# Float32r activation tiles of the 256-column products moved to byte 416 of a 512-byte block, on one Trainium2 core

## The chip, the cores and the metric

One Trainium2 chip, one of its cores, one launch of one program. The metric is device time in microseconds of that program, as the median of three runs. Parameters come from HBM, and the result goes back there.

## The reference

Two blocks in a row on 256 tokens of width 1024, in float32. The matrix products of both make up nearly all the work:

```
# first block
mod = silu(c) @ w_mod + b_mod                       # scale, shift, gate
h, hc = modulate(x, ...), modulate(ctx, ...)
q, k, v, g ... = split(h @ w_in)                    # retention and difference attention
x = x + mod[2] * (concat([ret, diff]) @ w_out)
h2 = modulate(x, ...)
x = x + mod[5] * peer_ffn(h2)                       # see below

# peer_ffn: 8 heads choose 16 of 128 * 128 experts for each token
q = h2 @ w_query;  s = q . sub_keys
experts, gate = top-k of the sums of two halves of s, softmax
act = gelu(expert_u[experts] . h2)
out = sum over the chosen: gate * act * expert_v[experts]

# second block, two layers
x = x + ((b * conv(c * u)) @ w_out)                 # layer 0: b, c, u = split(h @ w_in)
x = x + block_attention(h, keys and values of x)    # layer 1
x = x + softmax(q . k_mem) v_mem @ w_o              # both layers
x = x + (silu(h @ w_g) * (h @ w_u)) @ w_down        # both layers, 22 chunks of 128
out = rms_norm(x)
```

The peer layer is computed densely: all 16,384 experts are scored against all tokens, and the gates, zero for the experts that weren't chosen, are multiplied in.

## The kernel before, in words

Activations are kept transposed: a tile of [128, 8, 256] holds 8 chunks (`KC`) of 128 features on the partitions, and 256 tokens (`T`) along the free side. A float32 value is split into two float32r parts, `hi` (the cast) and `lo` (what the cast leaves), and a product of float32 matrices is three float32r products: hi by hi, weights' lo by hi, weights' hi by lo.

Weights come in blocks of [128, 1024]: one DMA on SyncE's queue into `raw` (`raw`), the cast to `whi` on ScalarE (L111) and the subtraction to `wlo` on VectorE or GpSimd (L115, `lo_plan` says which). `block` (L149) takes one such block, and `mm3` (L127) issues its 3 x 8 = 24 matmuls at L137, hi-hi for all chunks, then lo-hi, then hi-lo, all into one PSUM tile:

```
order = [(s, i) for s in range(3) for i in range(n)]
a, b = ((wh, xh), (wl, xh), (wh, xl))[s]
self.matmul = nc.tensor.matmul(out, a, b, start=..., stop=...)
```

The first operand, here 128 columns of weights, is loaded into the array (a record PEld of its own in the profile), the second, here the 256 tokens of one chunk, is streamed through it. Each matmul has a weight load of its own. Where a product is wanted with the tokens on the partitions (`natural_steps`, L172), the roles are turned round: 128 tokens of the activation are loaded, and 256 columns of weights are streamed. The expert sum of the peer (L942) streams 512 columns of weights over 128 tokens.

Stages follow each other in this order: conditioning and mixer (`mixer`, from the start to 310 us), peer (`peer`; queries and scores of the experts from 310, the filling of the slots by gates among the expert scores until 788, the expert sum until 1143), convolution (`conv_mixer`), memory attention (`mem_attn`), feed-forward (`swiglu`, L1275 ff.), block attention (`moba`), memory attention and feed-forward of layer 1. In between, steps of work for later stages (keys and values of the memory, `fill`) are handed out at places that a table names (`PLACES`, `at`).

The tiles that the change touches are the streamed activations: `hh`/`hl` of `gained` (L253), which the convolution, both memory attentions, both feed-forwards and the keys of the block attention stream; `h2h`/`h2l` in `peer`; `cath`/`catl` in `mixer`; `oh`/`ol` in `mem_attn` and `moba`; `ch`/`cl` in `conv_mixer`; `fh`/`fl` in `swiglu`; `hqh`/`hql` in `moba`. All are float32r, taken from pools one tile after another, and a matmul streams 1024 bytes of each partition at a time, so that all chunks of a tile start on the same byte of a 512-byte block. That byte is given by what the pools hold ahead of the tile: 256 for `hh`, `hl`, `fh`, `fl`, and for `oh`, `ol` of the memory attentions; 352 in the convolution (`hh`, `hl`, `ch`, `cl`); 288 for `hqh`, `hql` and the block attention's `oh`, `ol`; 384 for `cath`, `catl`; 224 for `h2h`, `h2l`. The weight tiles `whi` and `wlo` all start at byte 224 of such a block, as do their slices of 128 columns (512 bytes).

Of the kernel before, what the change touches and what calls it, by code (L numbers as in the profile page):

```python
# [16 lines left out]
F32R = mybir.dt.float32r  # L17
# [8 lines left out]
P = 128  # L26
T = 256
D = 1024
KC = 8
EPS = 1e-6  # L30
NCH = 128
NKC_FF = 22
# [31 lines left out]
ROUTE = 14, 15, 16  # L64
LOWEST = -3.0e38

G_NORM1, G_NORM2, G_MIX, G_MEM, G_MEMKV, G_FFN, G_KV, G_FINAL = 0, 1, 2, 4, 6, 8, 10, 11


class Build:  # L70
# [23 lines left out]
    def after(self, ins, other):  # L94
# [2 lines left out]
                               mybir.DependencyInfo(mybir.DependencyClass.NoSync, mybir.DependencyReason.DATA),  # L97
                               reason="order")


    def raw(self, src, pool=None, tag="raw", bufs=3):
        t = (pool or self.wpool).tile([P, 1024], F32, name=tag, tag=tag, bufs=bufs)
# [147 lines left out]
            nc.vector.scalar_tensor_tensor(h[1][:, k, cols], t, Bv[:, k:k + 1],  # L250
                                           h[0][:, k, cols].bitcast(F32), op0=OP.add, op1=OP.subtract)

    def gained(self, pool, x, gi, name="h"):  # L253

        hi = pool.tile([P, KC, T], F32R, name=name + "h", tag=name + "h", bufs=1)
        lo = pool.tile([P, KC, T], F32R, name=name + "l", tag=name + "l", bufs=1)
        for k in range(KC):
            self.gain_chunk(x[:, k], gi, k, hi[:, k], lo[:, k])
        return hi, lo
# [173 lines left out]
    def mixer(self):  # L433
        nc, io, tc = self.nc, self.io, self.tc
        with ExitStack() as ctx:
            self.banks(ctx, "mix")
            pool = self.pool(ctx, "mix")
# [55 lines left out]
            qk_g = self.load(pool, "qk_g", [P, 2])  # L493
            nc.vector.tensor_scalar(qk_g[:, 0:1], qk_g[:, 0:1], 0.125, None, op0=OP.mult)
            nc.vector.tensor_scalar(df_n, df_n, 1.0 - LAM_INIT, None, op0=OP.mult)
            cat = (pool.tile([P, KC, T], F32R, name="cath"), pool.tile([P, KC, T], F32R, name="catl"))

            toks = [(h[0][:, :, i * P:(i + 1) * P], h[1][:, :, i * P:(i + 1) * P]) for i in range(4)]

# [198 lines left out]
    def peer(self):  # L698
        nc, io = self.nc, self.io
        with ExitStack() as ctx:  # L700
# [1 line left out]
            big = self.pool(ctx, "slots")  # L702
            pool = self.pool(ctx, "peer")
            slots = big.tile([P, NCH, T], F32, name="slots")
            h = (pool.tile([P, KC, T], F32R, name="h2h"), pool.tile([P, KC, T], F32R, name="h2l"))
            space = slots[:, FREE:, :].rearrange("p c t -> p (c t)")
            at = [0]

# [412 lines left out]
    def mem_attn(self, l, kv):  # L1121
        nc, io = self.nc, self.io
        with ExitStack() as ctx:
            pool = self.pool(ctx, f"mem{l}")
            kT, v = kv
            h = self.gained(pool, self.x, G_MEM + l)
            cat = (pool.tile([P, KC, T], F32R, name="oh"), pool.tile([P, KC, T], F32R, name="ol"))
            r = None

            def query(hd):  # L1130
                nonlocal r
                o = self.psum([P, 2, T])
                q = pool.tile([P, 2, T], F32, name="q", tag="q", bufs=1)
                qh, ql = (pool.tile([P, 2, T], F32R, name="q" + c, tag="q" + c, bufs=3) for c in "hl")
                for i in range(2):
                    self.block(o[:, i], io["mem_wq"][l, 2 * hd + i], h, late=hd == i == 0)
                if hd == 0:
                    r = self.tracked_norm(pool, "nr", tables=l == 0)
                nc.vector.scalar_tensor_tensor(q, o, 1.0 / 16.0, r[:, None, :].to_broadcast([P, 2, T]),
                                               op0=OP.mult, op1=OP.mult)  # L1140
                nc.scalar.copy(qh, q)
                getattr(nc, QLO).tensor_sub(ql, q, qh)
                return qh, ql

            def weigh(hd, q):
                ps = []
                for tt in range(2):
                    s = self.psum([P, T], "sc")
                    t = slice(tt * P, (tt + 1) * P)
                    self.mm3(s, [(q[0][:, i, t], q[1][:, i, t], kT[0][:, 2 * hd + i], kT[1][:, 2 * hd + i])  # L1150
                                 for i in range(2)])
                    ps.append(self.softmax(pool, s, T, "ms"))
                return ps

            def turned(ps):
                pT = [pool.tile([P, 2, 2, P], F32R, name="pT" + c, tag="pT" + c, bufs=2) for c in "hl"]
                for tt, p in enumerate(ps):
                    tr = self.psum([P, 2, P], "aux")
                    for j in range(2):
                        nc.tensor.transpose(tr[:, j], p[:, j * P:(j + 1) * P], self.ident)  # L1160
                    nc.scalar.copy(pT[0][:, :, tt], tr)
                    nc.vector.tensor_sub(pT[1][:, :, tt], tr, pT[0][:, :, tt])
                return pT

            def apply(hd, pT):
                o = self.psum([P, 2, T], "aux")
                for i in range(2):
                    c = slice((2 * hd + i) * P, (2 * hd + i + 1) * P)
                    self.mm3(o[:, i], [(v[0][:, j, c], v[1][:, j, c], pT[0][:, j], pT[1][:, j]) for j in range(2)])
                nc.scalar.copy(cat[0][:, 2 * hd:2 * hd + 2], o)  # L1170
                nc.vector.tensor_sub(cat[1][:, 2 * hd:2 * hd + 2], o, cat[0][:, 2 * hd:2 * hd + 2])

            self.at(f"m{l}")
            qs = [query(0), query(1)]
            self.at(f"mq{l}")
            ps = weigh(0, qs[0])
            for hd in range(3):
                if hd < 2:
                    qs.append(query(hd + 2))
                self.at((f"mh{l}", hd))  # L1180
                pT = turned(ps)
                ps = weigh(hd + 1, qs[hd + 1])
                apply(hd, pT)
            self.at(f"me{l}")

            def rest():
                pT = turned(ps)
                yield
                apply(3, pT)

            self.residual_l(io["mem_wo"][l], cat, 6, rest())
# [27 lines left out]
    def conv_mixer(self, hook):  # L1219
        nc, io = self.nc, self.io  # L1220
        with ExitStack() as ctx:
            pool = self.pool(ctx, "conv")
            cw = self.load(pool, "conv_w", [P, KC, 3])
            h = self.gained(pool, self.x, G_MIX)
            cat = (pool.tile([P, KC, T], F32R, name="ch"), pool.tile([P, KC, T], F32R, name="cl"))

            def gate(m, o, b):
                cu = pool.tile([P, 2, T], F32, name="cu", tag="cu", bufs=2)
                nc.vector.tensor_mul(cu, o, r[:, None, :].to_broadcast([P, 2, T]))
                z = pool.tile([P, T], F32, name="z", tag="z", bufs=2)  # L1230
                nc.gpsimd.tensor_mul(z, cu[:, 0], cu[:, 1])
                y = pool.tile([P, T], F32, name="cy", tag="cy", bufs=2)
                nc.vector.tensor_scalar(y, z, cw[:, m, 2:3], None, op0=OP.mult)
                nc.vector.scalar_tensor_tensor(y[:, 1:], z[:, :T - 1], cw[:, m, 1:2], y[:, 1:],
                                               op0=OP.mult, op1=OP.add)
                nc.vector.scalar_tensor_tensor(y[:, 2:], z[:, :T - 2], cw[:, m, 0:1], y[:, 2:],
                                               op0=OP.mult, op1=OP.add)
                nc.gpsimd.tensor_mul(y, y, r)
                t = pool.tile([P, T], F32, name="ct", tag="ct", bufs=2)
                nc.vector.tensor_mul(t, b, y)  # L1240
                nc.scalar.copy(cat[0][:, m], t)
                nc.vector.tensor_sub(cat[1][:, m], t, cat[0][:, m])

            self.adder = getattr(nc, CADD)
            for k in range(KC):
                self.track(self.x[:, k], k)
            self.adder = nc.gpsimd
            for m in range(KC):
                self.at(("c", m))
                if m == HOOK:  # L1250
                    hook()
                o = self.psum([P, 2, T], "sc" if m < 2 else "mm")
                for i, c in enumerate((1, 2)):
                    self.block(o[:, i], io["conv_wi"][8 * c + m], h, late=m == i == 0)
                    if m == 1 and i == NORM1:
                        r = self.tracked_norm(pool, "nr", tables=True)
                b = self.psum([P, T])
                self.block(b, io["conv_wi"][m], h)
                if m == 0:
                    first = o, b  # L1260
                    continue
                if m == 1:
                    gate(0, *first)
                gate(m, o, b)
            self.at("ce")
            self.residual_l(io["conv_wo"], cat)

    def swiglu(self, l):
        nc, io = self.nc, self.io
        with ExitStack() as ctx:  # L1270
            pool = self.pool(ctx, f"ffn{l}")
            h = self.gained(pool, self.x, G_FFN + l)
            self.at(f"f{l}")
            act = (pool.tile([P, NKC_FF, T], F32R, name="fh"), pool.tile([P, NKC_FF, T], F32R, name="fl"))
            for m in range(NKC_FF):  # L1275
                o = self.psum([P, 2, T])
                for i in range(2):
# [58 lines left out]
    def moba(self):  # L1336
        nc, io = self.nc, self.io
        with ExitStack() as ctx:
# [34 lines left out]

            self.at("bk")
            kT = pool.tile([P, KC, T], F32, name="k")
            hq = [pool.tile([P, KC, T], F32R, name="hq" + c) for c in "hl"]

            def query(hd):
                return plain(io["moba_wq"][hd], hq, 128.0 ** -0.5)
# [9 lines left out]
                ahead = t  # L1389
                self.gain_chunk(self.x[:, hd], G_MIX + 1, hd, hq[0][:, hd], hq[1][:, hd])  # L1390

            cat = (pool.tile([P, KC, T], F32R, name="oh"), pool.tile([P, KC, T], F32R, name="ol"))

            def weigh(hd, q):
                ps = []
# [219 lines left out]
```

## Time and profile before

| | |
|---|---|
| median of 3 runs | 1922.86 us (1920.68 to 1924.4) |
| profiled execution, own time | 1923.66 us |
| its span | 1921.8 us |
| mean granted TensorE clock | 0.984 |
| TensorE busy | 1853.1 us (96%), 13488 matmuls |
| VectorE, ScalarE, GpSimd busy | 1329.4, 967.3, 538.4 us |
| DMA | 335.12 MB, mean 174 GB/s |

The profile shows one execution. PE is TensorE's matmuls, PEld its weight loads, DVE VectorE, ACT ScalarE, POOL GpSimd, SP SyncE. A matmul's record runs from its start until its last result is written and overlaps with the next ones, so that a mean of 280 ns says nothing of how fast they follow each other; that is read from starts, or from a stretch without idle time divided by its matmuls. The chain of waits goes back from the last instruction to what released it, or to the instruction ahead of it on its engine; asked for a stretch, it shows what ended that stretch.

### The profile page before, as it was taken

To read this page: it belongs to the slowest core of one execution; us is meant where nothing else is said; L and a number is where in the kernel's file an instruction comes from. 1 tells how busy PE (TensorE), PEld (TensorE's weight loads), DVE (VectorE), ACT (ScalarE), POOL (GpSimd) and SP (SyncE) were. 2 spreads that over 40 slices of the span, in tenths; PEclk is the share of its full clock that TensorE was granted. 3 is DMA by queue.
4 is the path that set the end of the run, shared out by engine and by line. 5 is a ranking of instruction groups with operands and counts; after the bars stand their busy time and mean duration, and the time that the engine had idled before them with its cause. 6 is when DMAs were issued, how large, how long until landed. Compare 5 with 4: busy or idle time off the path is not lost.

```text
span 1921.8 us, 34715 instructions
## 1 busy us (share of the span) xinstructions
PE 1853.1 (96%) x13488; PEld 1739.1 (90%) x13488; DVE 1329.4 (69%) x2594; ACT 967.3 (50%) x1517; POOL 538.4 (28%) x289
## 2 busy tenths in 40 slices
PE   6799999999999999999999998999999999999997
PEld 4697788999999999888888878999999998999997
DVE  8988965995555666765555568666765578767664
ACT  5655534445554444454544454455554545555453
POOL 2511115787666666200000004232000222110001
PEclk8999999999999999999999998999999999999999
DMA  7663434454444444655555555544555553535553
GB/s 262 219 229 119 134 131 158 165 186 166 155 148 153 150 154 154 242 188 195 196 189 196 195 196 171 185 160 150 196 189 187 187 175 117 176 114 190 190 188 121
DMA packets 99764, 335.12 MB, mean 174 GB/s; under 512 B 12400, under 2 KB 13456, under 8 KB 99216
## 3 DMA queue, kind: packets, MB, share of 16 engines
q1 hardware_dynamic: 98160, 330.68, 49.7%
q8 instruction: 106, 1.74, 0.4%
q10 hardware_dynamic: 1440, 2.23, 0.3%
q14 instruction: 58, 0.48, 0.1%
HBM read 329.59 MB, written 3.28 MB: 173 GB/s over the span
## 4 chain that ended last, share of the span: by engine, by line
PE 85%; DVE 8%; ACT 2%; issue 2%; DMA 2%; POOL 1%; SPq 0%; DVEq 0%; ACTq 0%; POOLq 0%
PE mm L137 52%; PE pair L942 18%; PE mm L172 4%; PE pair L879 3%; PE fill L172 2%; PE fill L137 2%; DVE wlo L115 1%; PE sc L137 1%; PE aux L137 1%; DVE mlo L115 1%; DMA mraw<-w_mod 0%; DVE roper L379 0%; DMA raw<-w_mod 0%; PE sc L614 0%; PE aux L619 0%
## 5 line engine op out<-in xcount | busy, mean ns | idle before, releaser
L111 ACT CAST whi<-raw 128x1024 fp32r<-128x1024 f32 x564 | 591.8, 1051 | 568.9 <-PE mm L137 294.0
L115 DVE TENSOR_TENSOR wlo<-raw,whi 128x1024 fp32r<-128x1024 f32 x389 | 487.3, 1254 | 283.1 <-PE pair L942 130.0
L115 POOL TENSOR_TENSOR wlo<-raw,whi 128x1024 fp32r<-128x1024 f32 x175 | 425.1, 2430 | 296.3 <-PE mm L137 195.6
L137 PE MATMUL mm<-hh,whi 128*128 128x256 f32 (+1 forms) x1184 | 179.9, 289 | 5.6 <-DVE ct L1240 4.4
L219 POOL TENSOR_TENSOR acc<-acc,accsq 128x256 f32<-128x256 f32 x42 | 40.1, 954 | 500.0 <-ACT accsq L217 500.0
L137 PE MATMUL mm<-hl,whi 128*128 128x256 f32 (+1 forms) x1184 | 176.8, 287 | 1.0 <-DVE hl L264 1.0
L137 PE MATMUL mm<-hh,wlo 128*128 128x256 f32 (+1 forms) x1184 | 175.9, 286 | 0.0
L137 PE MATMUL mm<-h2h,whi 128*128 128x256 f32 x1152 | 171.1, 291 | 4.1 <-ACT h2h L249 4.1
L137 PEld LDWEIGHTS mm<-hh,whi 128*128 128x128 f32 x1184 | 156.6, 190 | 10.6 <-issue 6.9
L137 PE MATMUL mm<-h2l,whi 128*128 128x256 f32 x1152 | 161.7, 283 | 0.0
L137 PE MATMUL mm<-h2h,wlo 128*128 128x256 f32 x1152 | 161.7, 283 | 0.0
L942 PE MATMUL pair<-whi,actl 128*128 128x512 f32 x512 | 158.2, 390 | 1.8 <-DVE actl L935 1.8
L942 PE MATMUL pair<-whi,acth 128*128 128x512 f32 x512 | 158.1, 390 | 0.7 <-ACT acth L934 0.7
L137 PEld LDWEIGHTS mm<-hl,whi 128*128 128x128 f32 x1184 | 155.4, 190 | 3.6 <-DVE hl L264 1.7
L137 PEld LDWEIGHTS mm<-hh,wlo 128*128 128x128 f32 x1184 | 155.3, 190 | 3.5 <-issue 1.5
L942 PE MATMUL pair<-wlo,acth 128*128 128x512 f32 x512 | 157.9, 389 | 0.2 <-DVE wlo L115 0.2
L137 PEld LDWEIGHTS mm<-h2h,whi 128*128 128x128 f32 x1152 | 149.8, 193 | 5.0 <-ACT h2h L249 4.8
L137 PEld LDWEIGHTS mm<-h2l,whi 128*128 128x128 f32 x1152 | 148.6, 192 | 0.0
L137 PEld LDWEIGHTS mm<-h2h,wlo 128*128 128x128 f32 x1152 | 148.6, 192 | 0.0
L863 DVE TENSOR_TENSOR ohA<-fill,selT 128x256 f32<-128x256 f32 x128 | 53.7, 420 | 94.5 <-PE pair L879 91.0
L942 PEld LDWEIGHTS pair<-whi,actl 128*128 128x128 f32 x512 | 95.7, 188 | 22.5 <-DVE actl L935 2.9
L942 PEld LDWEIGHTS pair<-wlo,acth 128*128 128x128 f32 x512 | 96.0, 188 | 20.7 <-DVE wlo L115 0.6
(408 smaller groups left out, 3165.6 us busy)
## 6 DMA issues: line engine op xcount, KB each, us to landing
raw<-peer_u SPq DMA_DIRECT2D x128, 512.0 KB, 3.5
raw<-peer_v SPq DMA_DIRECT2D x128, 512.0 KB, 3.5
raw<-ffn_gu SPq DMA_DIRECT2D x88, 512.0 KB, 3.5
raw<-ffn_dn SPq DMA_DIRECT2D x44, 512.0 KB, 3.5
raw<-w_mod SPq DMA_DIRECT2D x64, 256.0 KB, 3.9
raw<-conv_wi SPq DMA_DIRECT2D x24, 512.0 KB, 3.5
raw<-mem_wk SPq DMA_DIRECT2D x16, 512.0 KB, 4.5
mraw<-w_mod SPq DMA_DIRECT2D x16, 512.0 KB, 6.2
```

What stands on the lines that cost most here:

```text
L111: self.hi_copy = nc.scalar.copy(hi, raw)
L115: (nc.vector if plan == "v" else nc.gpsimd).tensor_sub(lo, raw, hi)
L137: self.matmul = nc.tensor.matmul(out, a, b, start=first and j == 0, stop=last and j == 3 * n - 1)
L172: self.matmul = nc.tensor.matmul(outs[i // 2][:, i % 2], a[:, k, :], b[:, w], start=k == 0 and s == 0 and i % 2 == 0, stop=k == 7 and s == ...
L219: self.adder.tensor_add(self.acc, self.acc, self.last)
L863: nc.vector.tensor_tensor(A, iota[:, None, :].to_broadcast([P, 2, P]), selT[:, 1, t:t + 2, None].to_broadcast([P, 2, P]), op=OP.is_equal)
L879: nc.tensor.matmul(o[:, 2 * j + i], A[:, i], Bt[:, i], start=True, stop=True)
L942: nc.tensor.matmul(acc[th][:, dh], x[:, tsl], wt[:, dh * 512:dh * 512 + 512], start=c == 0 and s == 0, stop=c == NCH - 1 and s == 2)
```

## The change

A helper `placed` takes a tile that is 128 elements (512 bytes) longer in each partition and hands out the part that begins `at` elements into it; the tiles named above come from it. With `at` x 4 bytes ahead, each of them starts on byte 416: 256 + 160, 352 + 64, 288 + 128, 224 + 192; for `cath` the room is 8 elements, which moves `catl` behind it by as much, 384 + 32 both. `hh`/`hl` of the mixer, streamed 512 columns at a time for the most part, stay at 224, as do the weights and the expert sum's activations. On all five engines' queues the instructions and their order are the same as before.

```
+ROOM = 128
+    def placed(self, pool, name, at, k=KC, room=ROOM, **kw):
+        t = pool.tile([P, k * T + room], F32R, name=name, **kw)
+        return t[:, at:at + k * T].rearrange("p (k t) -> p k t", k=k)
...
-    def gained(self, pool, x, gi, name="h"):
-        hi = pool.tile([P, KC, T], F32R, name=name + "h", tag=name + "h", bufs=1)
-        lo = pool.tile([P, KC, T], F32R, name=name + "l", tag=name + "l", bufs=1)
+    def gained(self, pool, x, gi, name="h", at=40):
+        hi = self.placed(pool, name + "h", at, tag=name + "h", bufs=1)
+        lo = self.placed(pool, name + "l", at, tag=name + "l", bufs=1)
...
-            cat = (pool.tile([P, KC, T], F32R, name="cath"), pool.tile([P, KC, T], F32R, name="catl"))
+            cat = self.placed(pool, "cath", 8, room=8), self.placed(pool, "catl", 0, room=0)
...
-            h = (pool.tile([P, KC, T], F32R, name="h2h"), pool.tile([P, KC, T], F32R, name="h2l"))
+            h = self.placed(pool, "h2h", 48), self.placed(pool, "h2l", 48)
...
-            cat = (pool.tile([P, KC, T], F32R, name="oh"), pool.tile([P, KC, T], F32R, name="ol"))
+            cat = self.placed(pool, "oh", 40), self.placed(pool, "ol", 40)
...
-            h = self.gained(pool, self.x, G_MIX)
-            cat = (pool.tile([P, KC, T], F32R, name="ch"), pool.tile([P, KC, T], F32R, name="cl"))
+            h = self.gained(pool, self.x, G_MIX, at=16)
+            cat = self.placed(pool, "ch", 16), self.placed(pool, "cl", 16)
...
-            act = (pool.tile([P, NKC_FF, T], F32R, name="fh"), pool.tile([P, NKC_FF, T], F32R, name="fl"))
+            act = self.placed(pool, "fh", 40, NKC_FF), self.placed(pool, "fl", 40, NKC_FF)
...
-            hq = [pool.tile([P, KC, T], F32R, name="hq" + c) for c in "hl"]
+            hq = [self.placed(pool, "hq" + c, 32) for c in "hl"]
...
-            cat = (pool.tile([P, KC, T], F32R, name="oh"), pool.tile([P, KC, T], F32R, name="ol"))
+            cat = self.placed(pool, "oh", 32), self.placed(pool, "ol", 32)
```

## Rows read from the trace of the kernel before

**Rows 1.** Page, parts 1 and 4: busy time by engine, chain that ended last.

```profile
PE 1853.1 (96%) x13488; PEld 1739.1 (90%) x13488; DVE 1329.4 (69%) x2594; ACT 967.3 (50%) x1517; POOL 538.4 (28%) x289
...
PE 85%; DVE 8%; ACT 2%; issue 2%; DMA 2%; POOL 1%; SPq 0%; DVEq 0%; ACTq 0%; POOLq 0%
PE mm L137 52%; PE pair L942 18%; PE mm L172 4%; PE pair L879 3%; PE fill L172 2%; PE fill L137 2%; DVE wlo L115 1%; PE sc L137 1%; PE aux L137 1%; DVE mlo L115 1%; DMA mraw<-w_mod 0%; DVE roper L379 0%; DMA raw<-w_mod 0%; PE sc L614 0%; PE
```

**Rows 2.** Busy time in stretches: peer's scores, slots filled, first feed-forward.

```profile
core 0: us, PE busy (x) PEld busy (x) DVE busy (x) ACT busy (x) POOL busy (x), PEclk, DMA share, GB/s
362.00:452.00 90.00, 90.00 (x753) 90.00 (x752) 82.00 (x321) 43.34 (x53) 72.93 (x32) 1.00 0.51 179
458.00:788.00 330.00, 330.00 (x2791) 329.96 (x2790) 201.12 (x491) 159.05 (x255) 226.74 (x95) 1.00 0.44 154
1345.00:1455.00 110.00, 110.00 (x945) 110.00 (x944) 76.61 (x103) 57.63 (x82) 0.00 (x0) 1.00 0.56 192
```

**Rows 3.** Chain within one stretch each (start us, us, what): pieces without a wait.

```profile
399.92 20.16 PE mm L137 x168
...
1342.98 117.14 PE mm L137 x1004
...
1730.38 117.72 PE mm L137 x1009
...
1635.97 17.80 PE mm L137 x151
...
1211.18 25.63 PE mm L137 x216
...
1541.91 10.18 PE mm L172 x86
```

**Rows 4.** Timeline of PE, 291.8 to 299.5 us (start us, us, what).

```profile
291.71 1.10 PE L137 MATMUL mm<-cath,wlo 128*128 128x256 f32 x8
...
298.28 1.10 PE L137 MATMUL mm<-catl,whi 128*128 128x256 f32 x8
299.22 0.50 PE L343 MATMUL mm<-ones,macc 128*128 128x2 f32 x4
```

**Rows 5.** Groups of PE by shape: one of three products each.

```profile
L137 PE MATMUL mm<-h2h,whi 128*128 128x256 f32 x1152 | 171.1, 291 | 4.1 <-ACT h2h L249 4.1
L137 PE MATMUL mm<-hh,whi 128*128 128x256 f32 x1136 | 165.8, 283 | 5.0 <-DVE ct L1240 4.4 <-ACT hh L263 0.6
...
L137 PE MATMUL mm<-fh,whi 128*128 128x256 f32 x352 | 50.3, 279 | 0.0
...
L137 PE MATMUL mm<-oh,whi 128*128 128x256 f32 x192 | 29.3, 285 | 0.7 <-ACT oh L1170 0.7
...
L137 PE MATMUL mm<-hqh,whi 128*128 128x256 f32 x64 | 11.2, 304 | 0.0
...
L137 PE MATMUL mm<-cath,whi 128*128 128x256 f32 x64 | 9.3, 284 | 0.7 <-ACT cath L628 0.7
L137 PE MATMUL mm<-ch,whi 128*128 128x256 f32 x64 | 9.2, 283 | 0.0
...
L137 PE MATMUL sc<-hh,whi 128*128 128x256 f32 x32 | 7.2, 337 | 2.1 <-ACT hh L263 2.1
```

**Rows 6.** Chain within a stretch: gate passes (128 columns), expert sum (512 columns).

```profile
600.46 0.89 PE pair L879 x8
...
802.40 24.97 PE pair L942 x108
```

**Rows 7.** Instructions on hh, ScalarE: convolution, then first feed-forward (ns min/median/max).

```profile
L263 ACT ACTIVATE hh<-x,gains x8: 491/493/507, 1145.7 to 1148.5; 128x256 fp32r<-128x256 f32 x8
...
L263 ACT ACTIVATE hh<-x,gains x8: 494/496/509, 1333.8 to 1337.4; 128x256 fp32r<-128x256 f32 x8
```

## The prediction

> **What bounds the kernel now.** I read the page's busy times and its chain first, then stretches of single stages, then the chain inside each stretch. TensorE is busy for 96% of the span, 85% of the chain that ended last is its own, and the line that the change feeds, L137, is 52% of that chain [rows 1]. In the stretches where L137 works, TensorE has no idle time at a granted clock of 1.00: 90 us of 90 in the peer's expert scores, 330 of 330 in the part where the slots are filled, 110 of 110 in the first feed-forward; VectorE, ScalarE and GpSimd have room there, the least being VectorE with 82 of 90 us [rows 2]. So a stage is as long as its matmuls are many, times the distance from one start to the next. That distance is the one quantity on which everything here rests; call it the pace. (A matmul's own duration of 280 to 290 ns overlaps with the next ones and tells nothing.)
>
> **What the pace hangs on.** Pace is a piece of the chain divided by its matmuls. All pieces below are streams of one form: 128 rows, 128 weight columns, 256 moving columns of float32r.
>
> The addresses are those that the program gives its tiles; the weight tiles whi and wlo start at byte 224 of a 512-byte block, and since steps are 512 bytes for the weights and 1024 for the activations, a stream keeps its byte throughout. I count the moving operand's byte minus the stationary one's, modulo 512:
>
> - offset 0 (peer, 224 on 224): 20.16 us for 168 [rows 3], 120.0 ns
> - offset 32 (feed-forwards, memory attentions, 256): 117.14 us for 1004 in the first feed-forward and 117.72 for 1009 in the second [rows 3], 116.7 ns both
> - offset 64 (the last projection of the block attention, 288): 17.80 us for 151 [rows 3], 117.9 ns
> - offset 128 (convolution, 352): 25.63 us for 216 [rows 3], 118.7 ns
> - offset 160 (the mixer's projection, 384): 64 starts from 291.71 to 299.22 us [rows 4], 117.3 ns
> - offset 480 (values of the block attention, where the weights stream over an activation at 256): 10.18 us for 86 [rows 3], 118.4 ns
>
> The pace thus differs by 3.3 ns with nothing else in the form changed, it is worst where both operands start on the same byte, and it does not rise or fall steadily with the offset. I read it as the next weight load and the running matmul getting in each other's way in SBUF, once per pair. The Trainium skill, "SBUF — State Buffer", section "Who interferes with whom", says otherwise: TensorE has one read port for the moving operand and an independent one for the weight load, and "PE and ACT never wait on anyone". By that rule the byte would not matter and the sum would be 0; the spread of 116.7 to 120.0 ns speaks against it, without proving the byte to be the cause, since each offset belongs to another stage. It is a rival below.
>
> **The change, part by part.** *Work.* No instruction is added, removed or put elsewhere on any engine, no DMA either, so no queue is passed and no wait added; costs can only come from addresses.
>
> *Writers.* ScalarE and VectorE now write the tiles at byte 416. ScalarE's eight casts take 493 ns (median) where the tile is at 352 and 496 at 256 [rows 7]; I cost the writers at nothing, and what would hide 3 ns is a ScalarE that is busy for 58 of 110 us [rows 2].
>
> *Matmuls that move to offset 192.* Each group has three products, so its count is three times the row of its first one [rows 5].
> - from offset 0: h2, 3 x 1152 = 3456
> - from 32: 896 of the 1136 + 32 rows of hh (the two feed-forwards 352 each, the two memory attentions and the block attention's keys 64 each), fh 352, and 128 of the 192 of oh: 3 x 1376 = 4128
> - from 128: the convolution's 192 of hh (32 of them in the other bank) and ch 64: 3 x 256 = 768
> - from 64: hqh 64 and the last 64 of oh: 3 x 128 = 384
> - from 160: cath 64: 3 x 64 = 192
>
> Together 8928. Weighted with their paces they now run at (3456 x 120.0 + 4128 x 116.7 + 768 x 118.7 + 384 x 117.9 + 192 x 117.3) / 8928 = 118.2 ns. With p for the new pace, the time is **1923.7 + 8.93 x (p - 118.2) us**, 1923.7 being the profiled execution's own time (span 1921.8); it stands 0.8 us above the median of 1922.9. I let every nanosecond count, as the stretches have no idle TensorE.
>
> *The new pace.* No stream of the trace has offset 192, so it is bounded. Upwards by the worst, 120.0 ns. Downwards by the eight passes of 128 columns between two blocks of the peer, which load as many weight columns and take 0.89 us [rows 6], 111 ns. Nearest are 160 and 128: from 118.7 to 117.3 the pace falls by 1.4 ns in 32 bytes. If the fall goes on it is 115.9 at 192, if it stops 117.3; I take the middle, **116.6 ns**. The terms: 3456 x -3.4 = -11.8 us, 4128 x -0.1 = -0.4, 768 x -2.1 = -1.6, 384 x -1.3 = -0.5, 192 x -0.7 = -0.1; together -14.4 us, 1909.3 for the profiled execution, 1908.5 against the median. I say 1909. The bounds give 1923.7 + 8.93 x 1.8 = 1939.8 and 1923.7 - 8.93 x 7.2 = 1859.4.
>
> "TensorE: Matmul & The Clock Gate" of the Trainium skill, section "Back-to-back issue gap", has a price of its own for an undisturbed stream, columns / 2.4 + 2.5 ns, which is 109.2 ns at 256 columns; by that estimate the sum would be -80 us. No stream of this width runs so fast here.
>
> *Matmuls that get another offset unasked.* In the block attention's values the tile at 416 is the stationary operand: 192 matmuls go from offset 480 to 320. Between 116.7 and 120.0 ns against 118.4 that is -0.3 to +0.3 us; I take nothing.
>
> *Matmuls that stay.* The expert sum streams 512 columns at offset 0, 24.97 us for 108 [rows 6], 231 ns with its stops, and neither its weights nor its activations change their byte.
>
> **The rivals.**
> 1. *A far better pace.* Offset 192 keeps the two operands apart long enough that the meeting falls away wholly or mostly: 111 to 115 ns, 1859 to 1895 us. For it: the passes of 128 columns need only 111 ns, so the weight load itself doesn't hold the pace at 117; against it: six offsets, and none under 116.7. If it came to the lower end, VectorE's 82 us would meet 83 us of TensorE in the stretch at 362 us [rows 2] and become its bound. Chance 0.27.
> 2. *No difference.* The paces belong to the stages and not to bytes, or offset 192 happens to give the present mean of 118.2: 1920 to 1927 us. For it: every pace was taken in a stage of its own, with other neighbours on the other engines. Against it: the two feed-forwards share one pace, and the convolution, with the same line and form, has another by 2 ns. The rule of the Trainium skill quoted above would make this the outcome. Chance 0.17.
> 3. *Slower, because 192 is one of the bad offsets.* The 3456 matmuls of the peer gain little and the 4128 from the best offset lose: the point from which this decides is a pace over 118.2; at 118.7 (the convolution's) it gives 1928 us, at 120.0 (the peer's now) 1939.8. For it: the paces jump between neighbours, 116.7 at 32 and 120.0 at 0; against it: only one of six offsets is over 118.7. Chance 0.16.
>
> **How the numbers follow.** My forecast, 115 to 117.8 ns, has the remaining 0.40; its own range is 1895 to 1920 us. A measurement of this kernel tells a difference from none at about 0.2%, 3.9 us, which is 0.43 ns of pace: faster is the forecast and rival 1, 0.67; the same is rival 2, 0.17; slower is rival 3, 0.16. The range takes the forecast, rival 1 almost to its lower bound, rival 2, and of rival 3 the part up to 118.9 ns: 1860 to 1930 us, which leaves out some 0.11 above and 0.07 below.
>
> **What would show it.** In the profile after, the chain's pieces in the peer, the feed-forward, the convolution and the mixer's projection should have one pace, 116.6 ns for the forecast: 24 matmuls of the peer in 2.80 us where 2.88 are needed now. The 512-column pieces and the counts must not change. If the stages keep their different paces at the same byte, the byte is not the cause and the reasoning is wrong from its root; if all have one pace but over 118.2 or under 115, the mechanism holds and the guess for offset 192 was off.

## The result and the profile after

The changed kernel takes 1906.91 us (median of 4 runs, 1898.9 to 1911.07) against 1921.84 us in the same comparison (4 runs): a ratio of 0.9916, 95% interval 0.9898 to 0.9934, or 15 us less. 1909 was forecast. A second comparison further down gives 0.9919 (0.9902 to 0.9936). The profiled execution is the fastest of the first four, 1898.9 us with a span of 1897.0.

The page of the changed kernel, parts 1 and 4 [rows 1 before; L143 is the former L137, since six lines came in ahead of it]:

```profile
PE 1830.2 (96%) x13488; PEld 1713.1 (90%) x13488; DVE 1324.2 (70%) x2594; ACT 968.1 (51%) x1517; POOL 541.2 (29%) x289
...
PE 86%; DVE 8%; ACT 2%; issue 2%; DMA 1%; POOL 1%; SPq 0%; DVEq 0%; ACTq 0%; POOLq 0%
PE mm L143 53%; PE pair L948 18%; PE mm L178 4%; PE pair L885 3%; PE fill L178 1%; PE fill L143 1%; DVE wlo L121 1%; PE sc L143 1%; PE aux L143 1%; ACT whi L117 1%; DMA mraw<-w_mod 0%; PE sc L546 0%; POOL wlo L121 0%; DMA raw<-w_mod 0%; DVE macc L361 0%
```

Same instructions, same bound: 23 us of TensorE's busy time are gone, while the other engines' moved by 5 us at most. Where they went is read from the chain in single stretches (start us, us, what), in this order: the peer's scores, the first feed-forward, the second one, the convolution, the mixer's projection, the block attention's last projection, and its values, where the tile at 416 is the stationary operand.

```profile
384.90 35.13 PE mm L143 x310
...
1329.95 120.13 PE mm L143 x1060
...
1709.92 120.13 PE mm L143 x1020
...
1195.89 23.91 PE mm L143 x211
...
276.97 11.90 PE mm L143 x101
...
1613.95 14.13 PE mm L143 x120
...
1517.93 9.07 PE mm L178 x80
```

Each piece divided by its matmuls: 113.3 ns in the peer (120.0 before [rows 3]), 113.3 in the first feed-forward but **117.8** in the second (both 116.7), 113.3 in the convolution (118.7), 117.8 in both projections (117.3 in the mixer's [rows 4], 117.9 in the block attention's), 113.4 for the values (118.4). So there isn't one pace at offset 192 but two, 113.3 and 117.8 ns, and the same code on the same byte has the one in the first layer and the other in the second. The peer's queries show where the choice is made. Between two blocks of 24 stand four short float32 passes, and the blocks alternate:

```profile
319.33 0.44 PE pair L745 x4
319.78 2.83 PE mm L143 x24
322.61 0.45 PE pair L745 x4
323.06 2.74 PE mm L143 x24
325.79 0.44 PE pair L745 x4
326.24 2.83 PE mm L143 x24
```

Every other block takes 2.83 us (starts 117 to 119 ns apart from first to last), the ones between 2.74 (120, 117, 116, then 114, 113, 113, 114, 113, 113 in a repeating pattern of three). A stream settles in one of two repeating patterns, "loops" from here on, when it starts, and keeps it to its end: 23 intervals or, in a feed-forward, over 1500. The choice isn't random everywhere: through the queries, and again through the slots, fast and slow streams alternate without an exception, which suggests that it depends on what ran ahead.

From the starts of the stages: the peer is 15.6 us shorter up to its expert sum, which gives back 1.3 (14.3 with it), the first feed-forward 5.2, the convolution 2.0. The second feed-forward takes as long as before: its stream is 1.7 us longer, and shorter waits ahead of it make up for that. Over all moved streams the mean pace in this execution is 115.3 ns (8574 intervals under 130 ns, so that stops are left out), and 8.93 x (115.3 - 118.2) = -25.9 us stands beside the 24.8 us by which the span fell.

### The profile page after: what moved, and what is told of

The parts are those of the page before. It is cut to its first block, busy times and chain, and to the rows that moved or that the text cites. A ratio compares the mean times of both kernels' runs of the same rounds, so it can differ in the third digit from the quotient of the medians.

```text
span 1897.0 us, 34717 instructions
## 1 busy us (share of the span) xinstructions
PE 1830.2 (96%) x13488; PEld 1713.1 (90%) x13488; DVE 1324.2 (70%) x2594; ACT 968.1 (51%) x1517; POOL 541.2 (29%) x289
## 4 chain that ended last, share of the span: by engine, by line
PE 86%; DVE 8%; ACT 2%; issue 2%; DMA 1%; POOL 1%; SPq 0%; DVEq 0%; ACTq 0%; POOLq 0%
PE mm L143 53%; PE pair L948 18%; PE mm L178 4%; PE pair L885 3%; PE fill L178 1%; PE fill L143 1%; DVE wlo L121 1%; PE sc L143 1%; PE aux L143 1%; ACT whi L117 1%; DMA mraw<-w_mod 0%; PE sc L546 0%; POOL wlo L121 0%; DMA raw<-w_mod 0%; DVE macc L361 0%
## 5 line engine op out<-in xcount | busy, mean ns | idle before, releaser
L143 PE MATMUL mm<-hh,whi 128*128 128x256 f32 (+1 forms) x1184 | 177.6, 287 | 6.5 <-DVE ct L1246 5.0
L143 PE MATMUL mm<-hl,whi 128*128 128x256 f32 (+1 forms) x1184 | 174.4, 285 | 0.9 <-DVE hl L270 0.9
L143 PE MATMUL mm<-hh,wlo 128*128 128x256 f32 (+1 forms) x1184 | 173.5, 285 | 0.6 <-DVE wlo L121 0.6
L143 PE MATMUL mm<-h2h,whi 128*128 128x256 f32 x1152 | 166.9, 287 | 4.1 <-ACT h2h L255 4.0
L143 PEld LDWEIGHTS mm<-hh,whi 128*128 128x128 f32 x1184 | 154.4, 190 | 12.0 <-issue 7.4
L143 PEld LDWEIGHTS mm<-hh,wlo 128*128 128x128 f32 x1184 | 153.4, 189 | 4.3 <-issue 1.5
L143 PEld LDWEIGHTS mm<-hl,whi 128*128 128x128 f32 x1184 | 153.5, 189 | 3.5 <-DVE hl L270 1.6
L143 PE MATMUL mm<-h2l,whi 128*128 128x256 f32 x1152 | 156.1, 278 | 0.0
L143 PE MATMUL mm<-h2h,wlo 128*128 128x256 f32 x1152 | 156.0, 278 | 0.0
L143 PEld LDWEIGHTS mm<-h2h,whi 128*128 128x128 f32 x1152 | 146.3, 191 | 5.0 <-ACT h2h L255 4.8
L143 PEld LDWEIGHTS mm<-h2l,whi 128*128 128x128 f32 x1152 | 143.1, 188 | 0.0
L143 PEld LDWEIGHTS mm<-h2h,wlo 128*128 128x128 f32 x1152 | 143.0, 188 | 0.0
L948 PEld LDWEIGHTS pair<-whi,acth 128*128 128x128 f32 x512 | 96.0, 188 | 20.7 <-ACT acth L940 1.0
```

The source lines that it names most:

```text
L143: self.matmul = nc.tensor.matmul(out, a, b, start=first and j == 0, stop=last and j == 3 * n - 1)
L948: nc.tensor.matmul(acc[th][:, dh], x[:, tsl], wt[:, dh * 512:dh * 512 + 512], start=c == 0 and s == 0, stop=c == NCH - 1 and s == 2)
```

## Experiments

Theory A: the pace of a stream hangs on the byte of the moving operand relative to that of the weights, and at 192 its start picks one of two loops. Rivals: the gain comes from longer or shifted tiles (B), or paces belong to stages (C).

**The peer alone.**

```
-    def gained(self, pool, x, gi, name="h", at=40):
+    def gained(self, pool, x, gi, name="h", at=0):
...        (cath, oh, ch, fh, hq likewise: at 0, tiles as long as in the changed kernel)
             h = self.placed(pool, "h2h", 48), self.placed(pool, "h2l", 48)
```

> Only the peer's two tiles are at byte 416 (offset 192 to the weights); all other tiles keep their bytes of before, in tiles as long as the changed ones. Theory A (the pace, start to start, hangs on the offset alone, and at offset 192 a stream settles in one of two loops, 113.3 or 117.8 ns, chosen where it starts): the peer gains 14.3 us as it did in the changed kernel, a pace mixed from both loops; all other stages keep their paces; 1907 us, give or take 3. Theory B (the gain comes from the tiles being longer or lying elsewhere, not from the byte): 1898 to 1907 us, with the feed-forwards gaining too, since their tiles are as long as in the changed kernel. Theory C (the pace belongs to the stage): no gain in the peer, 1922.

Measured: 1908.65 us, ratio 0.9927 (0.9901 to 0.9953). Chain in the peer's scores, then in the two feed-forwards:

```profile
399.99 20.06 PE mm L143 x177
...
1334.91 120.17 PE mm L143 x1030
...
1719.92 128.10 PE mm L143 x1098
```

113.3 ns in the peer, 116.7 in both feed-forwards, as before, though their tiles are as long as in the changed kernel. The length of the feed-forwards' tiles is not it.

**All but the peer.**

```
-            h = self.placed(pool, "h2h", 48), self.placed(pool, "h2l", 48)
+            h = self.placed(pool, "h2h", 0), self.placed(pool, "h2l", 0)
```

> The complement: the peer's tiles stay at byte 224 (offset 0), all others are at 416 as in the changed kernel. Theory A: the peer stays at 120.0 ns; the feed-forwards, each of them 1537 matmuls without a stop, are either at 113.3 ns (5.2 us less than before) or at 117.8 ns (1.7 us more), and the same whole; convolution and projections gain about 3 us; 1909 to 1923 us with runs that differ by some 7 or 14 us. Theory B (length or place of the tiles): the peer gains too. Theory C: 1922 in all runs.

Measured: 1920.0 us over 10 runs, 1911.48 to 1924.66, ratio 0.9987 (0.9969 to 1.0005): no difference that can be told. The peer and the feed-forwards of its profile:

```profile
399.93 20.16 PE mm L143 x168
...
1338.41 116.60 PE mm L143 x990
...
1724.21 123.90 PE mm L143 x1052
```

120.0 in the peer, and this time 117.8 ns in both feed-forwards: worse than the 116.7 that they had. The peer's own tiles are as long here as in the changed kernel, so that theory B fails for them too. Nearly all of the change's median gain is the peer's: 13.3 us (1921.96 - 1908.65) when it moves alone.

**All on the weights' byte.**

```
-    def gained(self, pool, x, gi, name="h", at=40):
+    def gained(self, pool, x, gi, name="h", at=120):
...        (the others likewise, so that each tile starts on byte 224)
```

> All the moved tiles start at byte 224 as the weights do, offset 0. Theory A: every stream of L143 has the peer's old pace of 120.0 ns in the feed-forwards, the convolution and the projections too: 4128 x 3.3 + 768 x 1.3 + 384 x 2.1 + 192 x 2.7 ns and 0.3 us for the values of the block attention, 16 us more than before: 1938 us. Theory B: as the changed kernel, 1899 to 1911. Theory C: 1922, each stage with its pace of before.

Measured: 1935.58 us, ratio 1.0068 (1.0046 to 1.009), 13.6 us more than before where 16 were expected. Convolution and the two feed-forwards:

```profile
1214.19 22.92 PE mm L143 x191
...
1347.52 107.51 PE mm L143 x896
...
1739.55 108.47 PE mm L143 x904
```

120.0 ns in all three, where 118.7 and 116.7 stood. That settles theory C: the peer's old pace comes with its byte into the other stages. The four runs lie close together (1934.44 to 1937.58), which fits a single loop at offset 0, but doesn't show it: the four at offset 32 further down, where there are two loops, are hardly further apart (1911.3 to 1914.67).

**A sweep of offsets.** One tile of weights, one of activations, no other engine at work:

```
+        for d in range(32):
+            for n in STOPS:                              # 1, 2, 3, 4 float32 matmuls ahead
+                stop(n)
+                last = stream(4 * d, COUNT, act, T, ...)  # 48 matmuls, 16 * d bytes past the weights' byte
```

> Not the reference's work: one tile of weights, one of activations, and streams of 48 matmuls of 256 columns (24 of 512 columns for the second part) at each offset from 0 to 496 bytes in steps of 16 (of 32 for 512 columns), with 1, 2, 3 or 4 float32 matmuls ahead of each stream so that it starts in another phase. Theory A: 120 ns at offset 0, 116.7 (or 117.7) at 32, 117.8 at 64, 118.7 at 128, 117.3 at 160, 118.4 at 480, and at 192 two values, 113.3 and 117.8, by the stream's start; offsets not yet seen have paces between 111 and 120. Theory C: one pace for all offsets. For 512 columns, 227 ns at offset 0, and 216 to 227 elsewhere if the same holds there.

Pace in ns over the second half of each stream, for its four starts (at offset 0 the four streams ran on into each other, 192 matmuls with one start; at 256 four separate starts all give 120.0):

```
offset       0              16                      32                      48
       120.0 all   118.7 116.7 113.3 118.7  116.7 117.8 116.7 116.7       118.3 all
offset      64              80                      96                     112
  113.3 117.8 117.8 117.8  118.3 120.0 120.0 118.3  120.0 all            113.3 all
offset     128             144                     160                     176
  120.0 120.0 118.7 118.8  118.7 118.8 116.7 116.7  117.3 117.5 118.8 117.4  119.2 all
offset     192             208                     224                     240
  113.3 117.8 117.8 113.3  119.2 all               118.3 all       117.1 117.0 117.3 117.0
```

From 256 to 496 the same row comes again within 0.1 ns, but for two offsets: at 288 the values of 32 come in another order, and at 272 the 113.3 that one start met at 16 isn't met. So the period is 256 bytes, not 512. Every value of the kernel's trace is here (120.0 at 0, 116.7 at 32, 117.8 at 64, 118.7 at 128, 117.3 at 160, 118.3 at 224, which is 480), though the weights lie on another byte and the other engines are idle. And 112 is new: the fast loop from every start. How it is reached, in the chain: the four streams at 112, then the four at 192, with the passes of 128 columns between them (0.22 us for each float32 matmul).

```profile
183.65 5.50 PE sah L53 x48
...
189.60 5.50 PE sah L53 x48
...
195.77 5.49 PE sah L53 x48
...
202.15 5.50 PE sah L53 x48
```

```profile
307.78 5.46 PE sbc L53 x48
313.24 0.44 PE stop L45 x4
313.68 5.66 PE sbc L53 x48
319.34 0.67 PE stop L45 x6
320.01 5.66 PE sbc L53 x48
325.67 0.89 PE stop L45 x8
326.56 5.46 PE sbc L53 x48
```

At 112 a stream first goes through about ten matmuls at 116 to 121 ns and then falls into 113, 113, 114; at 192 it is 5.46 or 5.66 us by the start. For 512 columns the sweep gives 226.7 ns at offset 0, 228.9 at 64 and 232.6 to 234.3 at the other offsets tried: the widest products stand best where they stand, and the expectation that they would gain elsewhere was wrong.

**More starts, and the weights on another byte.** Theory A2 is theory A as the sweep leaves it: the pace hangs on the offset modulo 256.

```
-        w = pool.tile([P, 1024], F32R, name="whi")
+        room = pool.tile([P, 1024 + 128], F32R, name="whi")
+        w = room[:, WAT:WAT + 1024]                      # WAT = 40: byte 32 of 256
```

> Not the reference's work: streams of 48 matmuls at offsets 0, 32, 64, 112 and 192, eight starts each (1 to 8 float32 matmuls ahead), and the weight tile at byte 32 of a block of 256 instead of 128. Theory A2: the same paces as in the sweep at the same offsets: 120.0 at 0 from all starts, 116.7 or 117.8 at 32, 113.3 or 117.8 at 64 and 192, 113.3 at 112 from all starts. If the absolute byte counted: other paces.

Offset 0: 120.0 in all eight streams (five starts, since the first four ran on into each other); 32: 116.7 from all; 64: 117.8 from all; 112 and 192: 113.3 from all. The paces are those of the sweep, so it is the relative byte that counts for them. Which loop a stream takes at 32, 64 or 192 isn't told by the number of passes ahead of it: at 192 two of four starts were slow with the weights on byte 128, none of eight on byte 32; at 64 one of four was fast, and none of eight. What picks the loop stays open, and the weights' own byte may have a part in that.

**Offset 112 in the kernel.** The sweep points to a version that should beat both:

```
-            h = self.placed(pool, "h2h", 48), self.placed(pool, "h2l", 48)
+            h = self.placed(pool, "h2h", 28), self.placed(pool, "h2l", 28)
-    def gained(self, pool, x, gi, name="h", at=40):
+    def gained(self, pool, x, gi, name="h", at=20):
...        (oh, fh 20; ch 124; hq and the block attention's oh 12; cath and catl on byte 80 and 336)
```

> As the changed kernel, but with all moved tiles at byte 336 (the hi part of the mixer's projection at byte 80): offset 112 to the weights modulo 256, where the sweep of offsets fell into the 113.3 ns loop from all of its starts, within some ten matmuls. Theory A2 (the pace hangs on the offset modulo 256; at 192 a stream's start picks 113.3 or 117.8 ns, at 112 there is only 113.3): all 8928 matmuls at 113.3 ns and some 0.05 us at each start, 80 starts or so: 1923.7 + 8.93 x (113.3 - 118.2) + 4 = 1884 us, runs within a few us of each other, both feed-forwards at 113.3 in the profile. Theory A1 (in the whole kernel the other engines' accesses or DMAs upset the loop, and the sweep on an idle core does not carry over): paces between 113 and 118, 1890 to 1912 us.

Measured: **1892.21 us**, ratio 0.9845 (0.9831 to 0.9858), 5 runs from 1889.59 to 1895.07. Queries, scores, first and second feed-forward:

```profile
320.10 2.78 PE mm L143 x24
322.89 0.44 PE pair L745 x4
323.33 2.78 PE mm L143 x24
...
384.97 35.13 PE mm L143 x310
...
1329.97 120.13 PE mm L143 x1060
...
1709.95 120.13 PE mm L143 x1060
```

Both feed-forwards run at 113.3 ns, and each block of the queries takes 2.78 us. That is no better than 2.74 and 2.83 in turn, since each start costs about 55 ns (22 intervals at 115.8 instead of 113.3 ns). In the peer, with 84 starts, the mean pace is 114.7 ns against 115.2 in the changed kernel, some 2 us; the larger part of the gain lies in the long streams. The 8 us that are missing to the 1884 expected: 130 streams instead of 80 are some 3 us, and the expert sum, whose bytes are as before, took 359.6 us from its first to its last matmul, where it was 355.1 before. That can't be put down to offset 112: in the other profiles it took between 356.4 us (the changed kernel) and 359.1 (all on the weights' byte). TensorE's waits in it for ScalarE's and VectorE's tiles are longer (5.3 us against 2.7 before); why was not tried.

**Offset 32 everywhere.**

```
-    def gained(self, pool, x, gi, name="h", at=40):
+    def gained(self, pool, x, gi, name="h", at=0):
...        (peer 8, convolution 104, block attention 120, projection of the mixer 96: byte 256)
```

> All moved tiles at byte 256, offset 32 to the weights, which was the best pace seen before the change. Theory A2: 116.7 or 117.8 ns by a stream's start, in the peer too (120.0 before): 3456 x -3.3 (or -2.2), 768 x -2 (or -1) and 0.3 us from the others: 1910 to 1915 us, that is most of the gain of the changed kernel in a typical run. If the byte 416 itself mattered: 1922.

Measured: 1912.26 us, ratio 0.9954 (0.9939 to 0.9968). Peer's scores and first feed-forward:

```profile
384.89 35.12 PE mm L143 x301
...
1339.91 110.13 PE mm L143 x944
```

116.7 ns both. The byte 416 has no virtue of its own; another byte gives 9.2 us (1921.45 before, in the same comparison), over half of what the change gives, and as before the gain sits where offset 0 is left.

**The changed kernel again.**

> The changed kernel once more, for the spread of its runs on the chip of the others. Theory A2: each feed-forward is at 113.3 or at 117.8 ns as a whole, 7 us apart, so the runs lie between 1896 and 1913 us, further apart than those of the kernel at offset 112; the profile need not show the loops of the first one (first feed-forward 113.3, second 117.8).

Measured: 1905.85 us, ratio 0.9919 (0.9902 to 0.9936), 6 runs from 1900.89 to 1911.31; in the same comparison offset 112 spans 5.5 us, this one 10.4. Its two feed-forwards:

```profile
1329.94 120.13 PE mm L143 x1020
...
1715.93 114.13 PE mm L143 x969
```

Both at 117.8 ns here; in the first profile one was at 113.3. A feed-forward is about 1537 matmuls, so its loop decides over 1537 x 4.5 ns = 6.9 us. That the loops make the spread of the runs is argued, not shown, since one run of each kernel has a trace. The feed-forwards can't be all of it: with both of them at 117.8 ns the profiled run, 1904.68 us, is faster than three of the other five. Other streams change their loop too: both projections are at 113.3 ns here and were at 117.8 in the first profile.

## Why the prediction was right, and where it was not

1909 us was forecast and 1906.9 measured, on the side that was forecast, inside the likeliest case's own range of 1895 to 1920.

- *The bound and the formula* (time by number of matmuls times pace, every nanosecond counting) held. The profiled execution's mean pace of 115.3 ns gives -25.9 us, the span shows -24.8; with all on the weights' byte +16 was expected and +13.6 came.
- *The cause.* That the pace hangs on the offset between the two operands is shown: the peer's 120.0 ns went into the feed-forwards with the byte, and an otherwise idle core repeats the whole list. Rival 2's ground (paces belong to stages) is refuted. That the weight load and the matmul hinder each other in SBUF is still only my reading: no run took the load away. The Trainium skill ("SBUF — State Buffer", section "Who interferes with whom") gives TensorE two independent read ports and says that it never waits for anyone. What the prediction took from this, that the byte would not matter, doesn't agree with 113.3 to 120.0 ns by the byte alone; whether it is the ports that differ isn't shown.
- *The new pace* was the step that failed, though the time came out. The prediction put one pace of 116.6 ns, halfway between a falling line from 118.7 over 117.3 and a level one. There is no such line: neighbours 16 bytes apart are at 120.0 and 113.3, and offset 192 has two paces, 113.3 and 117.8. That the time came out is luck in the size: a mix of two loops, near half and half in both profiles of the changed kernel, lands about where the guess was. By the prediction's own test (all stages at one pace) the picture was incomplete; by its other test (stages that share a byte but keep their old paces) it was not wrong, since the mixes don't follow the old paces. The trace of before held a sign of it. The prediction costed all of offset 32 with the feed-forwards' 116.7 ns, but the projection of the second memory attention, on the same byte 256, runs at 117.8 (kernel before, start us, us, what):

```profile
1703.93 14.13 PE mm L137 x120
```

- *The terms.* The peer's matmuls were to give 11.8 us and gave 15.6; the convolution 1.6 and gave 2.0. The feed-forwards were to give next to nothing (-0.1 ns), but each gives 5.2 us or costs 1.7; of the six in the three profiles that have them at offset 192, one gives.
- *The range* reached to 1860 for a pace of 111 ns. The 0.07 that it is said to leave out below is too much beside that, as rival 1's own price ends at 1859. Rival 1 (111 to 115 ns) was half right: the fast loop at 113.3 lies in it, and at 112, where no stream was seen to keep another loop, the kernel's 1892 us lie in its 1859 to 1895. The Trainium skill's "TensorE: Matmul & The Clock Gate", section "Back-to-back issue gap", gives its columns / 2.4 + 2.5 ns for a matmul on its own, not for a stream of weight loads and matmuls. The 109.2 ns that follow from it were not met at any of the 32 offsets.
- *Rival 3* (192 is one of the bad offsets) is half right as well: in the profile with all but the peer moved, the feed-forwards lose 1.1 ns at the new byte.
- *The values of the block attention* were put at nothing; 192 x -5 ns in the profile, 1 us at most. Their offset 320 is 64 by the period of 256, where the sweep has 113.3 and 117.8.
- *Writers at nothing* held: ScalarE's busy time is 968.1 us, 967.3 before, and VectorE's 1324.2, 1329.4 before.

## What to carry to other kernels

Where TensorE has no idle time, divide a stretch of the chain by its matmuls: if streams of one form have different paces, compare the bytes of their two operands before anything else. Move tiles by 16 bytes at a time in a sweep on an idle core, with several starts for each byte; take the offset that is fast from all of them, not the one that is fast once, and weigh the start's toll where streams are short. The list of paces here is for float32r and 256 columns. A kernel whose runs lie further apart after a change may have a pace with two loops, and one profile then shows one of several outcomes.

## What was not expected of the hardware

- The pace repeats every 256 bytes of relative offset, in steps as fine as 16 bytes: 120.0 ns at 96 and 113.3 at 112.
- Streams settle in periodic patterns (113, 113, 114 ns at the fast one), with two or three different ones at some offsets, and stay there for over 1500 matmuls, with other engines at work.
- At 512 columns the order is another: 226.7 ns at offset 0, whose 120.0 ns is the slowest pace met at 256 columns, and up to 234.3 elsewhere.
